# Expert rows summed by group in PSUM with one-hot products instead of through memory

## The chip, the cores and the metric

One Trainium2 chip, one of its cores. The time is the device time of one execution in microseconds (us). The trace is of one profiled execution; PE is the matrix engine, DVE, ACT and POOL are the vector, scalar and GpSimd engines, SP issues most DMAs.

## The reference, cut to what matters

One encoder layer (Hyena and HGRN2 mixers, an output projection, a mixture of experts, a final norm) on 1024 tokens and 16 meta tokens, width 1024, all float32. The change lies in the experts and in what follows them. 64 experts stand in 8 groups of 8; a token goes to the two best experts of its best group, so both its experts are in one group.

```python
# h: tokens after the mixers; hf = rms_norm(h) * gain
g_sel = argmax(hf @ w_rg);  top 2 of the 8 experts of that group, gates p_group * p_top / sum(p_top)
y_e   = (silu(xe @ w_gate[e]) * (xe @ w_up[e])) @ w_down[e]        # 1024 -> 512 -> 1024
out   = rms_norm(h + sum over the token's two experts of gate * y_e) * norm_final
```

Each expert has three matrices of 2 MB, 403 MB in all. They are read once.

## The kernel before, in words

The mixers take the first 780 us and are not touched. Then come three stages.

Routing (`choose`, `route`, `rows_out`, `gates`). The last output projection is woven with the choice of experts. Each of the eight 128-token tiles of h goes to memory (`rdr`, L1180) with its rsqrt factor in an extra column. `route` makes, with one-hot bf16 products on PE, a table of 64 slots for each expert: which row to fetch (`tab.src`) and where to put the result (`tab.dst`).

Experts (the loop at L1735). For expert x, POOL fetches its rows by an indirect DMA (`xg`, L1345, five buffers): partitions 0 to 63 hold the first halves of 64 rows, 64 to 127 the second halves. PE transposes them (`xt`), multiplies gate and up side by side in the two column halves (`gu`, L1367: 16 float32 matmuls, which the trace records as two passes each), ACT scales, PE transposes (`ht`, L1372), ACT and DVE make silu times up (L1374, L1375), PE multiplies with w_down (`y`, L1385: 8 matmuls, two passes each), DVE copies, and POOL writes the rows by an indirect DMA to `yd` in memory (L1388). PE works in order: gu(x), ht(x), with xt(x+1) between, y(x), gu(x+1).

The matrices come in 2 MB transfers on SP's queue (L1320, L1328) into nine buffers, in the order gate, up, down. A transfer is issued when the second before it has landed (`AHEAD` = 2) and its buffer is free. The first seven are issued while the routing still runs; the eighth waits for the second row fetch to land ("rows first").

End (`overflow`, `final`). All engines read `over` and skip the branch for experts with more than 64 rows, which is not taken here. Then the 8 MB of `yd` are read back in eight tiles, each tile is summed with h by the gates (on PE for four tiles, on DVE for four), ACT sums the squares, POOL makes the rsqrt in six small operations, DVE scales, and SP writes the result.

## Time and profile before

| | us |
|---|---|
| median of 3 runs | 1871.41 (1870.23 to 1877.0) |
| the profiled execution, its own time | 1871.61 |
| its span | 1869.9 |
| routing ends, the eighth matrix is issued | 849.93 |
| the last matrix has landed, about | 1815.7 |
| end of the span | 1869.9 |

| in the span | PE | DVE | ACT | POOL |
|---|---|---|---|---|
| busy | 86% | 43% | 24% | 11% |

A row of a timeline has start, duration, engine, line, operation and tiles, and how many such instructions are merged in it; in square brackets stands the idle time before and what ended it. SPq and POOLq are the queues of those engines. A row of windows has the busy time of each engine in that stretch with its instructions, then PE's granted clock (1 is 2.4 GHz), the busy share of the 16 DMA engines and GB/s. A row of groups has total busy time and mean ns of one instruction.

### The profile page before, as it was taken

The numbers are of one execution on the slowest core, as the hardware profiler recorded it, in microseconds if no ns is written. First come the engines' busy times: TensorE is split into PE (matmuls) and PEld (weight loads), VectorE is DVE, ScalarE is ACT, GpSimd is POOL, SyncE is SP. The second block draws the span as 40 slices with busy tenths as digits, with TensorE's granted clock in tenths as the row PEclk, the third lists the DMA queues.
The fourth block names the chain that finished last, engine by engine and source line by source line (L and its number), as shares of the span: only waits on it lengthen the run. The fifth ranks groups of instructions, "written<-read, shape, count | busy, mean of one in ns | idle before, by whom it ended". The sixth has DMA issues, their size and how long they took to land. (4 is left out here: it accounts for less than half of the span.)

```text
span 1869.9 us, 23041 instructions
## 1 busy us (share of the span) xinstructions
PE 1615.8 (86%) x8931; PEld 988.5 (53%) x8931; DVE 812.5 (43%) x1633; ACT 455.6 (24%) x871; POOL 203.5 (11%) x271
## 2 busy tenths in 40 slices
PE   5999999989998898998988888888888888888885
PEld 3998988878886676873332222222222232223232
DVE  6688879869889785671111111111111111111114
ACT  5443346353454552231000000000000000000001
POOL 0011000000100001002111111111111111111004
PEclk9999999999998898998999999999999999999997
DMA  5376766676745526468999999999999999999987
GB/s 168 94 225 196 233 194 201 206 223 195 212 161 179 181 72 151 160 271 355 424 420 419 420 418 420 421 421 421 422 420 420 417 420 419 421 422 416 412 357 283
DMA packets 150057, 574.55 MB, mean 307 GB/s; under 512 B 20468, under 2 KB 85072, under 8 KB 124153
## 3 DMA queue, kind: packets, MB, share of 16 engines
q1 hardware_dynamic: 122840, 511.30, 69.3%
q0 software_dynamic: 25808, 57.00, 10.4%
q10 hardware_dynamic: 1296, 4.75, 0.6%
q8 instruction: 71, 1.16, 0.2%
q14 instruction: 42, 0.34, 0.1%
HBM read 532.79 MB, written 57.02 MB: 315 GB/s over the span
## 5 line engine op out<-in xcount | busy, mean ns | idle before, releaser
L1367 PE MATMUL gu<-w,xt 128*64 128x512 f32 x2048 | 516.0, 604 | 76.3 <-DMA w<-in_w_up 75.5
L1367 PEld LDWEIGHTS gu<-w,xt 128*64 128x64 f32 x2048 | 167.6, 139 | 407.9 <-issue 278.9
L1362 DVE TENSOR_TENSOR xt<-xt,gain 128x512 f32<-128x512 f32 x64 | 44.2, 691 | 526.6 <-PE gu L1367 489.1
L1385 PE MATMUL y<-w,ht 128*64 128x512 f32 x1024 | 236.4, 602 | 25.8 <-DVE ht L1375 25.4
L1369 ACT ACTIVATE gu<-gu,xg 128x512 f32<-128x512 f32 x64 | 44.0, 687 | 849.3 <-PE gu L1367 849.3
L496 PE MATMUL w<-ah,wh 128*128 128x346 f32 (+2 forms) x672 | 233.4, 348 | 0.7 <-ACT ah L248 0.7
L496 PE MATMUL w<-al,wh 128*128 128x346 f32 (+2 forms) x672 | 234.0, 348 | 0.0
L496 PE MATMUL w<-ah,wl 128*128 128x346 f32 (+2 forms) x672 | 232.9, 348 | 0.0
L1385 PEld LDWEIGHTS y<-w,ht 128*64 128x64 f32 x1024 | 69.4, 137 | 151.0 <-issue 112.1
L1387 DVE COPY y<-y 128x512 f32<-128x512 f32 x64 | 44.2, 691 | 241.5 <-PE y L1385 241.5
L496 PEld LDWEIGHTS w<-ah,wh 128*128 128x128 f32 x672 | 128.3, 191 | 11.0 <-issue 1.6
L496 PEld LDWEIGHTS w<-ah,wl 128*128 128x128 f32 x672 | 128.5, 192 | 9.9 <-issue 1.6
L496 PEld LDWEIGHTS w<-al,wh 128*128 128x128 f32 x672 | 128.4, 191 | 9.0 <-issue 1.2
L1345 POOL DMA_INDIRECT xg<-rdr,src x64 | 65.6, 1024 | 485.0 <-ACT gu L1369 474.7
L1388 POOL DMA_INDIRECT yd<-y,dst x64 | 65.1, 1017 | 371.1 <-DVE y L1387 368.2
L1372 PE MATMUL ht<-ident,gu 128*128 128x128 f32 x256 | 47.7, 309 | 50.2 <-ACT gu L1369 50.1
L1372 PEld LDWEIGHTS ht<-ident,gu 128*128 128x128 f32 x256 | 35.6, 208 | 103.1 <-ACT gu L1369 103.1
L1375 DVE TENSOR_TENSOR ht<-ht 128x256 f32<-128x256 f32 x64 | 27.0, 421 | 94.8 <-ACT ht L1374 86.4
L498 ACT ACTIVATE pc<-w 128x346 f32<-128x346 f32 (+2 forms) x84 | 41.9, 499 | 72.2 <-PE w L496 67.1
L462 PE MATMUL h<-fh,ftab 128*128 128x256 f32 x256 | 53.0, 288 | 4.7 <-ACT fh L449 3.6
L486 ACT CAST wh<-w 128x512 fp32r<-128x512 f32 x64 | 39.5, 620 | 63.0 <-PE w L496 56.4
L1360 PE MATMUL xt<-ident,xg 128*128 128x128 f32 x256 | 42.9, 290 | 11.5 <-DMA xg<-rdr,src 10.5
(427 smaller groups left out, 2269.0 us busy)
## 6 DMA issues: line engine op xcount, KB each, us to landing
w<-in_w_gate SPq DMA_DIRECT2D x64, 2048.0 KB
w<-in_w_down SPq DMA_DIRECT2D x63, 2048.0 KB
w<-in_w_up SPq DMA_DIRECT2D x62, 2048.0 KB
w<-in_w_in SPq DMA_DIRECT2D x64, 256.0 KB
ftab<-in_tab POOLq DMA_DIRECT2D x32, 384.0 KB, 4.3
tab<-in_tabf POOLq DMA_DIRECT2D x16, 768.0 KB, 5.8
tab<-in_tabi POOLq DMA_DIRECT2D x16, 640.0 KB
kdr<-V SPq DMA_DIRECT2D x16, 512.0 KB
```

Source lines behind the costliest of these rows:

```text
L462: nc.tensor.matmul(A[-1][:, z * HC:z * HC + HC], lhs, rhs, start=i == 0, stop=i == len(prods) - 1)
L496: nc.tensor.matmul(pt[:, :n], lhs[k // 4][:, k % 4, :], rhs[:, k, c0:c0 + n], start=i == 0, stop=i == 3 * KT - 1)
L498: nc.scalar.activation(dst[:, c0:c0 + n], pt[:, :n], func)
L1345: d = nc.gpsimd.indirect_dma_start(out=xg, out_offset=None, in_=rows, in_offset=bass.IndirectOffsetOnAxis(ap=src, axis=0), bounds_check=2 ...
L1360: nc.tensor.transpose(pt[:, j].rearrange("p h s -> p (h s)"), xg[:, j:512:4], e.ident)
L1362: nc.vector.tensor_mul(xt, pt, gain[:, :, :, None].to_broadcast([P, 4, 2, SLOTS]))
L1367: nc.tensor.matmul(pg[64 * z:64 * z + 64], xt[:, j, h], w[:, h, j], start=i == 0, stop=i == 7)
L1369: nc.scalar.activation(gu, pg, AF.Copy, scale=xg[:, 512:513])
L1372: nc.tensor.transpose(pu[:, j].rearrange("p h s -> p (h s)"), gu[:, j::4], e.ident)
L1385: nc.tensor.matmul(py[64 * z:64 * z + 64], ht[:, j], wdv[:, j, z], start=j == 0, stop=j == 3)
L1387: nc.vector.tensor_copy(y, py)
L1388: nc.gpsimd.indirect_dma_start(out=ydv, out_offset=bass.IndirectOffsetOnAxis(ap=dst, axis=0), in_=y, in_offset=None, bounds_check=4 * SEQ ...
```

## The change

Weights: gate and up of an expert lie side by side in memory, one run of 32 KB for each partition, and come as one 4 MB transfer into one of three buffers; w_down has three buffers of 2 MB. The order is gate+up, down, expert by expert; the last four are gate+up 62 and 63, down 62 and 63. Four transfers (14 MB, as before) are issued ahead of "rows first".

Results: `expert_add` multiplies an expert's result by its gates and adds h itself for a token's first expert (`res`), splits it in two float32r parts (`yh`, `yl`), and 8 one-hot float32r products of 64 rows each (`hot`) add it to the group's sums in PSUM (two tiles of 128 tokens, four banks). Four of the eight stand after gu of the next expert, four after its `ht`; xt(x+1) and then y(x) follow. After the eighth expert of a group `group_out` normalises the sums (rsqrt by 13 small DVE operations) and POOL writes them to the result by token. `yd`, its reading back and `final` remain only in the branch for overflow, which now stands at the very end.

Tables: `group_tables`, after `gates`, makes the place of each slot in its group, its gate, whether it is the token's first expert, and the token of each place. The PSUM tiles gu, ht and y have one buffer each (two before).

```diff
     oh, m = first_max(e, rp, gl, c.rev, "g")
+    nc.vector.tensor_copy(c.G[:, ts], oh)
     t4 = rp.tile([P, n, 8, 8], F32, name="t4", bufs=1)
...
+GROUP = 256
+
+
+def group_tables(e, ps, rp, kp, c, tab):
+
...
+    Gf = c.G.rearrange("p t g -> p (t g)")
+    pg = ps.tile([P, 512], F32, name="t")
+    nc.tensor.matmul(pg[:, :64], c.tri, Gf, start=True, stop=False)
+    for i in range(1, 8):
+        nc.tensor.matmul(pg[:, i * 8:64], c.ones, Gf[:, :(8 - i) * 8], start=False, stop=i == 7)
...
+    def by_slot(values, out, first, last):
+
+        r = rp.tile([P, 2, 8, NE], BF16, name="rg", bufs=2)
+        for k in range(2):
+            nc.vector.tensor_mul(r[:, k], c.E[:, k], values[k][:, :, None].to_broadcast([P, 8, NE]))
+        for k in range(2):
+            for t in range(8):
+                nc.tensor.matmul(out, c.hot[:, k, t], r[:, k, t], start=first and k + t == 0, stop=last and k + t == 8)
+
+    pq = ps.tile([P, 512], F32, name="f")
+    by_slot((q[:, 1], q[:, 1]), pq[:, :NE], True, True)
+    tab.q = e.room[0][:, :NE]
+    nc.vector.tensor_scalar(tab.q, pq[:, :NE], -1.0, None, op0=ALU.add)
...
+    for i in range(3):
+        part = rp.tile([P, 2, 8], BF16, name="gp", bufs=2)
+        nc.vector.tensor_copy(part, rem if i else c.w)
+        if i < 2:
+            nc.vector.tensor_sub(rem, rem if i else c.w, part)
+        by_slot((part[:, 0], part[:, 1]), pw[:, :NE], i == 0, i == 2)
+    tab.ws = e.room[0][:, NE:]
+    nc.vector.tensor_copy(tab.ws, pw[:, :NE])
...
+    pt = ps.tile([P, 512], F32, name="f")
+    for h in range(GROUP // P):
...
+        hq = rp.tile([P, 2, 8, NE], BF16, name="rg", bufs=2).rearrange("p k t x -> p (k t x)").rearrange("p (t c) -> p t c", c=P)
+        nc.vector.tensor_tensor(hq, places[:, None, :].to_broadcast([P, 8, P]), qh[:, :, None].to_broadcast([P, 8, P]),
+                                op=ALU.is_equal)
+        for t in range(8):
+            nc.tensor.matmul(pt[:, 16 * h:16 * h + 16], hq[:, t], rt[:, t].rearrange("p j g -> p (j g)"),
+                             start=t == 0, stop=t == 7)
...
 AHEAD = 2
 XB = 5
-RD = 7
-ORDER = (2, 3, 0, 5, 1, 7, 8, 4, 6)
...
+RD = 4
+GU = [("gu", x) for x in range(NE)]
+DN = [("d", x) for x in range(NE)]
+LOADS = GU[:2] + DN[:1] + GU[2:3] + DN[1:3] + [l for x in range(3, NE - 2) for l in (GU[x], DN[x])] + GU[NE - 2:] + DN[NE - 2:]
...
+    kind, x = LOADS[i]
+    if kind == "gu":
+        w = pools["gu"][x % 3].tile([P, 2, 2, 4, 512], F32, name="wgu")
+        src = I["w_gu"][x]
+        if x == NE - 1:
+            for h in range(2):
+                d = nc.sync.dma_start(w[:, h], src[:, h])
         else:
-            d = nc.sync.dma_start(w, src)
+            d = nc.sync.dma_start(w.rearrange("p h z j f -> p (h z j f)"), src.rearrange("p h z j f -> p (h z j f)"))
...
+        w = pools["d"][x % 3].tile([P, 2, 4, 512], F32, name="w")
         if x == NE - 1:
-            nc.sync.dma_start(dst[:, 0], src[:, 0])
-            d = nc.sync.dma_start(dst[:, 1], src[:, 1])
+            src = I["w_down"][0, x].rearrange("(p h j) c -> p h (j c)", h=2, j=2)
+            for h in range(2):
+                d = nc.sync.dma_start(w[:, h].rearrange("p j f -> p (j f)"), src[:, h])
...
     nc = e.nc
     pt = ps.tile([P, 4, 2, SLOTS], F32, name="xt")
     for j in range(4):
-        nc.tensor.transpose(pt[:, j].rearrange("p h s -> p (h s)"), xg[:, j:512:4], e.ident)
+        last = nc.tensor.transpose(pt[:, j].rearrange("p h s -> p (h s)"), xg[:, j:512:4], e.ident)
     xt = xp.tile([P, 4, 2, SLOTS], F32, name="xt")
     nc.vector.tensor_mul(xt, pt, gain[:, :, :, None].to_broadcast([P, 4, 2, SLOTS]))
+    return xt, last
+
+
+def expert_hidden(e, ps, xp, wgu, xg, xt, between=None):
+
+    nc = e.nc
     pg = ps.tile([P, 512], F32, name="gu")
     for i in range(8):
         h, j = divmod(i, 4)
-        for z, w in enumerate((wg, wu)):
-            nc.tensor.matmul(pg[64 * z:64 * z + 64], xt[:, j, h], w[:, h, j], start=i == 0, stop=i == 7)
+        for z in range(2):
+            last = nc.tensor.matmul(pg[64 * z:64 * z + 64], xt[:, j, h], wgu[:, h, z, j], start=i == 0, stop=i == 7)
     gu = xp.tile([P, 512], F32, name="gu")
     nc.scalar.activation(gu, pg, AF.Copy, scale=xg[:, 512:513])
     pu = ps.tile([P, 4, 2, SLOTS], F32, name="ht")
-    for j in range(4):
-        nc.tensor.transpose(pu[:, j].rearrange("p h s -> p (h s)"), gu[:, j::4], e.ident)
+    with ExitStack() as order:
+        if between:
+            with e.tc.issue_after(last.ins):
+                last = between(0)
+            order.enter_context(e.tc.issue_after(last.ins))
+        for j in range(4):
+            last = nc.tensor.transpose(pu[:, j].rearrange("p h s -> p (h s)"), gu[:, j::4], e.ident)
+    if between:
+        with e.tc.issue_after(last.ins):
+            between(1)
     ht = xp.tile([P, 4, SLOTS], F32, name="ht")
     nc.scalar.activation(ht, pu[:, :, 0], AF.Silu)
     nc.vector.tensor_mul(ht, ht, pu[:, :, 1])
...
+def expert_add(e, ps, xo, wd, ht, xg, x, tab, acc):
+
+
+    nc = e.nc
+    wdv = wd.rearrange("p h j f -> p (h j f)").rearrange("p (j z c) -> p j z c", j=4, z=2)
+    one = slice(x, x + 1)
+    res = xo.tile([P, 512], F32, name="res", bufs=2)
+    nc.vector.tensor_scalar(res, xg[:, :512], tab.first[:, one], None, op0=ALU.mult)
+    hot = xo.tile([P, GROUP], F32R, name="hot", bufs=2)
+    nc.vector.tensor_scalar(hot, e.places, tab.q[:, one], None, op0=ALU.is_equal)
+    py = ps.tile([P, 512], F32, name="y")
+    for j in range(4):
+        for z in range(2):
+            nc.tensor.matmul(py[64 * z:64 * z + 64], ht[:, j], wdv[:, j, z], start=j == 0, stop=j == 3)
+    nc.vector.scalar_tensor_tensor(res, py, tab.ws[:, one], res, op0=ALU.mult, op1=ALU.add)
+    yh = xo.tile([P, 512], F32R, name="yh", bufs=2)
+    nc.scalar.copy(yh, res)
+    yl = xo.tile([P, 512], F32R, name="yl", bufs=2)
+    nc.vector.tensor_sub(yl, res, yh.bitcast(F32))
+
+    def products(c):
+        for z in range(2):
+            r = slice(64 * z, 64 * z + 64)
+            for i, y in enumerate((yh, yl)):
+                last = nc.tensor.matmul(acc[c][:, z], hot[r, c * P:c * P + P], y[r], start=x % 8 + i == 0, stop=x % 8 == 7 and i == 1)
+        return last
+    return products
+
+
+def group_out(e, xo, acc, gain, tok, out):
+
+    nc = e.nc
+    n = GROUP // P
+    ss = xo.tile([P, n], F32, name="fs")
+    for c in range(n):
+        junk = xo.tile([P, 2, 512], BF16, name="fj")
+        nc.scalar.activation(junk, acc[c], AF.Square, accum_out=ss[:, c:c + 1])
+    r = rsqrt(e, xo, ss, D)
+    for c in range(n):
+        y = xo.tile([P, 2, 512], F32, name="fo", bufs=2)
+        nc.vector.scalar_tensor_tensor(y, acc[c], r[:, c:c + 1], gain, op0=ALU.mult, op1=ALU.mult)
+        nc.gpsimd.indirect_dma_start(out=out, out_offset=bass.IndirectOffsetOnAxis(ap=tok[c], axis=0),
+                                     in_=y.rearrange("p h c -> p (h c)"), in_offset=None, bounds_check=SEQ - 1, oob_is_err=False)
+
...
+        ch.close()
+        xh = pool(c6, "xh", 2)
         xp = pool(c6, "xp", 2)
...
+        xo.tile([P, 3360], mybir.dt.uint8, name="pad")
+        gu = [pool(c6, "gu1"), pool(c6, "gu0")]
+        dn = [pool(c6, "d1")] + [pool(c6, f"d{i}", side="right") for i in (0, 2)]
+        gu.append(pool(c6, "gu2", side="right"))
+        we = {"gu": [gu[1], gu[0], gu[2]], "d": [dn[1], dn[0], dn[2]]}
+        e.wdma, e.W = [], {}
+        at = 0
+        for at in range(RD):
+            expert_weights(e, we, at)
...
             rdv = rdr.rearrange("t h c -> (t h) c")
-            ydv = yd.rearrange("t k (h c) -> (t k h) c", h=2)
...
+            e.places = xo.tile([P, GROUP], F32, name="places")
+            nc.gpsimd.iota(e.places, pattern=[[1, GROUP]], base=0, channel_multiplier=0, allow_small_or_imprecise_dtypes=True)
+            fgain = xo.tile([P, 2, 512], F32, name="fg")
+            nc.scalar.dma_start(fgain.rearrange("p h c -> p (h c)"), I["norm_final"].rearrange("(o d) -> o d", o=1).to_broadcast([P, D]))
+            accs, due = {}, {}
+
+            def close(x, c):
+
+                last = due[x](c)
...
+            def down(x, ht):
+                g = x // 8
+                if g not in accs:
+                    accs[g] = [ps.tile([P, 2, 512], F32, name="acc") for _ in range(GROUP // P)]
+                due[x] = expert_add(e, ps, xo, e.W["d", x], ht, rows[x][0], x, tab, accs[g])
+
+            hts = {}
+            xt, _ = expert_rows(e, ps, xh, rows[0][0], gain)
             for x in range(NE):
-                while len(W) < min(3 * x + 9, 3 * NE):
-                    W.append(expert_weights(e, we, len(W)))
+                while at < min(2 * x + 6, 2 * NE) or x >= NE - 2 and at < 2 * NE:
+                    expert_weights(e, we, at)
+                    at += 1
+                hts[x] = expert_hidden(e, ps, xh, e.W["gu", x], rows[x][0], xt, (lambda c: close(x - 1, c)) if x - 1 in due else None)
+                if x < NE - 1:
+                    xt, last = expert_rows(e, ps, xh, rows[x + 1][0], gain)
...
-                    late.append(expert_hidden(e, ps, xp, W[g], W[g + 1], rows[x][0], gain))
+                    with tc.issue_after(last.ins):
+                        down(x, hts.pop(x))
                 if x + XB < NE:
                     rows.append(fetch(e, xp, tab.src[:, x + XB:x + XB + 1], rdv, False))
-            for x, ht in zip((NE - 2, NE - 1), late):
-                expert_out(e, ps, xp, W[2 * NE + x], ht, tab.dst[:, x:x + 1], ydv)
-        c6.close()
+                if x == 4:
+                    over = nc.values_load(tab.over[0:1, 0:1], min_val=0, max_val=8 * SEQ)
+            for x in (NE - 2, NE - 1):
+                down(x, hts.pop(x))
+            for x in (NE - 2, NE - 1):
+                for c in range(2):
+                    close(x, c)
+        op = Room([we["gu"][i].tile([P, 2, 2, 4, 512], F32, name="wgu").rearrange("p h z j f -> p (h z j f)") for i in range(3)]
+                  + [we["d"][i].tile([P, 2, 4, 512], F32, name="w").rearrange("p h j f -> p (h j f)") for i in range(3)])
+        ydv = yd.rearrange("t k (h c) -> (t k h) c", h=2)
         with ExitStack() as c2:
-            overflow(e, psum(c2, xt=1, gu=1, ht=1, y=1), pool(c2, "op"), tab, gain, rdv, ydv)
-        fps = ctx.enter_context(tc.tile_pool(name="fps", bufs=1, space=PSUM, reuse_waits="tile"))
-        final(e, pool(ctx, "fp", 2), fps, hres, yd, tab.w, out)
+            ps = psum(c2, xt=1, gu=1, ht=1, y=1)
+            with tc.If(over > 2 * GROUP):
+                overflow(e, ps, op, tab, gain, rdv, ydv)
+                final(e, op, rdr, yd, tab.w, out)
 
 
```

## Rows read from the trace of the kernel before

**Rows 1.** Windows: the stretch in which experts are loaded, and the end behind it.
```profile
849.93:1815.70 965.77, 812.67 (x3554) 301.66 (x3556) 113.76 (x190) 69.85 (x129) 126.07 (x124) 0.99 1.01 419
1815.70:1869.90 54.20, 29.68 (x78) 11.65 (x74) 23.48 (x27) 8.83 (x16) 19.79 (x50) 0.79 0.64 250
```
**Rows 2.** Waits of SP's queue, 900 to 1800 us: total us, times, longest.
```profile
SPq L1320 <- DMA w<-in_w_up: 286.0, 57, 6.2
SPq L1328 <- DMA w<-in_w_gate: 262.4, 57, 5.4
```
**Rows 3.** Timeline of SP's queue: two issues of matrices, one after the other.
```profile
1302.48 0.33 SPq L1320 DMA_DIRECT2D w<-in_w_up  x1
1307.34 0.33 SPq L1328 DMA_DIRECT2D w<-in_w_down  x1
```
**Rows 4.** Timeline of PE: one round of the expert loop while weights are ahead.
```profile
877.49 6.18 PE L1367 MATMUL gu<-w,xt 128*64 128x512 f32 x28
883.59 0.75 PE L1360 MATMUL xt<-ident,xg 128*128 128x128 f32 x4
884.53 0.74 PE L1372 MATMUL ht<-ident,gu 128*128 128x128 f32 x4 [0.18 <-ACT gu L1369]
885.20 1.08 PE L1367 MATMUL gu<-w,xt 128*64 128x512 f32 x4
886.20 3.65 PE L1385 MATMUL y<-w,ht 128*64 128x512 f32 x16
889.68 1.89 PE L1367 MATMUL gu<-w,xt 128*64 128x512 f32 x8
```
**Rows 5.** Timeline, first and last of 32 float32r products; group of their weight loads.
```profile
812.86 0.48 PE L1058 MATMUL f<-woll,ygh 128*128 128x512 f32 x1
820.05 0.39 PE L1058 MATMUL f<-wohl,ygl 128*128 128x512 f32 x1
...
L1058 PEld LDWEIGHTS f<-wohl,ygl 128*128 128x128 f32 x32 | 6.0, 188 | 1.2
```
**Rows 6.** Timeline: from gu to y within one expert.
```profile
1305.36 0.74 PE L1372 MATMUL ht<-ident,gu 128*128 128x128 f32 x4 [0.83 <-ACT gu L1369]
...
1307.04 3.65 PE L1385 MATMUL y<-w,ht 128*64 128x512 f32 x16 [0.45 <-DVE ht L1375]
```
**Rows 7.** Groups by line: total busy us, mean ns, idle before and its releasers.
```profile
L1045 DVE TENSOR_TENSOR wol<-hres,woh 128x512 fp32r<-128x512 f32 x8 | 5.1, 677 | 0.0
...
L1044 ACT CAST woh<-hres 128x512 fp32r<-128x512 f32 x8 | 4.6, 619 | 5.9 <-DMA hres<-in_w_out 5.9
...
L1518 ACT ACTIVATE fj<-f 128x1024 bf16<-128x1024 f32 x4 | 4.1, 1019 | 9.9 <-PE f L1512 8.6 <-POOL rqx L152 1.3
...
L1521 DVE SCALAR_TENSOR_TENSOR fo<-f,rqy,fg 128x1024 f32<-128x1024 f32 x4 | 5.1, 1284 | 6.4 <-POOL rqy L157 6.3
...
L123 DVE TENSOR_TENSOR rqt<-rqy 128x4 f32<-128x4 f32 x12 | 1.9, 159 | 0.2
```
**Rows 8.** Timeline: from the routing into the experts.
```profile
844.04 0.17 DVE L1237 TENSOR_TENSOR wts<-wts,low 128x8 f32<-128x8 f32 x1
...
846.53 1.02 POOL L1345 DMA_INDIRECT xg<-rdr,src  x1 [0.30 <-issue]
...
849.93 0.34 SPq L1320 DMA_DIRECT2D w<-in_w_up  x1
...
850.46 8.89 PE L1367 MATMUL gu<-w,xt 128*64 128x512 f32 x32 [0.78 <-DVE xt L1362]
...
863.26 0.33 SPq L1320 DMA_DIRECT2D w<-in_w_up  x1
```
**Rows 9.** Timeline: the last two y, the last store of POOL, the last scaling.
```profile
1814.68 7.09 PE L1385 MATMUL y<-w,ht 128*64 128x512 f32 x32
...
1823.18 0.99 POOL L1388 DMA_INDIRECT yd<-y,dst  x1 [2.85 <-DVEq L1399]
...
1864.17 1.28 DVE L1521 SCALAR_TENSOR_TENSOR fo<-hres,rqy,fg 128x1024 f32<-128x1024 f32 x1 [1.09 <-POOL rqy L157]
```

## What the change will do to the time, predicted blind

> **What bounds the kernel now.** I read four views in this order. The windows by stage come first: from 849.93 us to about 1815.7 us the 16 DMA engines are busy throughout at 419 GB/s, while PE is busy 813 of 966 us, and the last 54.2 us run at 250 GB/s with little of anything [rows 1]. The waits of SP's queue say that this middle stretch is bound by the transfers: nearly every issue waits for an earlier matrix to land, not for a buffer [rows 2]. The timeline of that queue gives the pace of a matrix alone: 4.86 us for 2.097 MB, 431 GB/s [rows 3]. The timeline of PE where weights are ahead gives its own pace: 889.68 - 877.49 = 12.2 us for an expert [rows 4]. The three matrices of an expert take 14.6 us alone, and 965.8 us / 185 matrices x 3 = 15.66 us as measured [rows 1]. So DMA sets the stretch, and PE has some 3 us to spare for each expert. Behind the stretch nothing overlaps: finish y, write `yd`, read it back, sum, normalise, store.
>
> **The change part by part.** The sum is made on the profiled execution: span 1869.9 us, its own time 1871.61, so 1.7 us lie around the span; the median of the runs is 0.2 us lower.
>
> *The stretch of the weights.* 185 matrices at 4.86 us are 899 us of the 965.8; the other 67 us go to the indirect rows. By the code these are 1024 tokens x 2 experts x 4 KB = 8.4 MB of fetches and as much of `yd`, some 16.1 MB within the stretch: 241 GB/s, dearer than a matrix [rows 1, 3]. The change takes `yd` away and adds 4.2 MB of result rows, of which seven groups, 3.7 MB, fall into the stretch. Priced by its bytes at 431 GB/s `yd` is 19 us; if all the dearness is its own, 67 - 18 = 49 less what fetches cannot avoid, so I take half of 67, 34 us, as the upper end, and 25 as the value. The new stores cost 9 to 15 us, I take 11: their rows are 4 KB where those of `yd` were 2 KB. Net -14 us, bounds -25 and -4.
> One 4 MB transfer for two of 2 MB: a matrix alone already runs at 431 GB/s with the next one queued behind it, and DMA shows no idle time, so I cost it at nothing; what covers its start is the transfer before it, at least 4.86 us [rows 1, 3]. The Trainium skill, "DMA: Bandwidth & Descriptors", section "Anatomy of one DMA", gives each DMA a fixed 2 us, which would promise 128 us for 64 DMAs fewer; the rows show no such gap between two matrices, so the sum has none of it; by the page it would be 1703 us, to which the trace leaves no chance worth a number.
>
> *PE in the stretch.* An expert gains 8 products of 64 rows x 512 columns, float32r, and no other PE work. Such a shape is not in the trace; the nearest is the float32r product with 128 rows, (820.05 - 812.86) / 31 = 0.232 us each, its weight load of 0.188 us hidden [rows 5]. That makes 1.86 us; if the two row halves ran side by side, 0.93; if weight loads were not hidden, 8 x 0.42 = 3.4. I take 1.86. A change of operand shape also costs: a pair of gu passes over 512 columns takes 6.10 / 14 = 0.436 us, so four transposes of 128 columns about as much, an estimate; from 884.53 to the next gu at 885.20 it is 0.67, so 0.24 us [rows 4]. There are two such changes per expert now and five after: +0.7 us. From the 12.2 us goes the wait of 0.5 us of `ht` for ACT, which the first four products now fill (0.83 us between the end of gu and `ht`), and from `ht` to y there are 1.7 us, filled by four products and xt(x+1) [rows 4, 6]. So 12.2 - 0.5 + 1.9 + 0.7 = 14.3 us per expert, bounds 13.2 and 16. The DMA gives 64 experts about 959 us from the first gu to the last y (sum below), 15.0 each. PE stays just under; that margin, 0.7 us of 15, is the tightest point of this forecast. On DVE an expert gains four passes over 128 x 256 to 512 at up to 0.7 us and on ACT one of 0.62 [rows 7]: 3 us and 1.7 us of 15, off the path. `group_out` puts some 8 us on ACT and DVE once in eight experts; its sums must be free when the next group's first products come, a round later: it just fits, and a slip costs a few us per group on PE only. On POOL two stores per group stand ahead of later fetches, which have five buffers, so four rounds, of lead.
>
> *The start.* `choose` and `route` gain five small DVE operations (0.2 us) where DVE is full: +1 us on the way to "rows first". `group_tables` is twelve times a 128 x 512 pass of 0.68 us and some 15 small ones of 0.16 to 0.2: 11 us of DVE [rows 7]. Some runs in gaps; I put 9 us behind the gates, ready at 844.04. Before, gu(0) starts at 850.46 [rows 8]; after, it waits for DVE until about 853.5, bounds 850 and 859. It takes 8.9 us, to 862.4. The third gate+up buffer is full by then, so the next transfer waits for gu(0) to end, and the queue runs dry at 863.26, when before the second of the two matrices issued at 850 lands [rows 8]. So up to 4 us of delay are covered by those two matrices; I take +4 us in all for a cover that frays, bounds 0 and +10.
>
> *The end.* With T the landing of the last matrix, about 1815.7 before, the last y ends at T + 6.1 [rows 9]. After, y of expert 63 waits for the sum of 62 to be read (one PSUM buffer): T + 7. Then one by one: scale and add 0.7, cast 0.62, difference 0.68 and hand-offs (T + 9.3), four products 0.9 (T + 10.2), two sums of squares at 1.02 + 0.2 (T + 12.7), 13 small operations at about 0.2 (T + 15.3), two scalings of 1.28 (T + 17.9) [rows 5, 7]. The store is indirect, on POOL; the last one before goes from 1865.45 to 1869.9, 4.4 us, by SP [rows 9]. I take 5 us and 0.6 for the branch: T + 23.5, bounds 20 and 28, in place of 54.2 [rows 1]. Net -30.7, bounds -34 and -26.
>
> **Sum.** 1869.9 + 4 - 14 - 30.7 = 1829.2 us of span, and 1.7 around it: **1831 us**. The bounds added up give 1813 and 1851.
>
> **The rivals.**
> *PE becomes the bound, slower than before.* The products do not hide their weight loads, because each half of the rows is used twice running: 8 x 0.188 = 1.5 us more per expert, a cycle of 15.8. The end is then 853.5 + 64 x cycle + 16.5 (from the last y) + 1.7. At 15.8 it is 1883; with 0.2 us more for the five changes of shape, 1896. It decides from a cycle of 15.0, and the kernel is slower than before from 15.62. For it: no 64-row product of this width is in the trace, and the margin is thin. Against: 31 products in a row hid loads of the same size [rows 5], and the rounds have two places in which PE waits today. Two pages stand for it. The Trainium skill, "TensorE: Matmul & The Clock Gate", section "Part 3: Packing small matmuls", lets a weight load overlap a running matmul only in another row group; the rows differ, since full-height loads are hidden at 0.232 us. "TensorEngine Tiling (Array Packing)" of the skill, section "Key Properties", says that a change of tiling mode drains the engine; the 0.24 us agrees in kind.
> *PE slightly over.* Cycle 15.0 to 15.5: 1832 to 1864, say 1850.
> *The start starves.* The tables hold gu(0) until 859 and the fetches slip by 3 us: +10 in place of +4 and no more, since afterwards the transfers run on: 1837; with half the gain of `yd`, 1845.
> *The large transfers help.* If matrices ran at 4.86 us less what the fetches disturb, and stores cost nothing, another 15 us go: about 1815.
>
> **How the numbers follow.** Forecast (DMA stays the bound) 0.74, within 1815 to 1846; start and rows dearer, 1845 to 1855, 0.06; PE slightly over 0.09; PE the bound and slower 0.07; below 1815 0.04. The range 1814 to 1857 leaves out the slow case and the edges. A difference under 0.5% (9 us, 1862 to 1881) cannot be told from no change here. Faster 0.89: the forecast, the start, the large transfers and half of PE slightly over; same 0.04; slower 0.07.
>
> **What would show it.** Right: DMA share still 1.0 from 850 us to about 1806, SP's queue waiting for matrices, PE waiting for gate+up once per expert, products at 0.23 us or less, 22 to 25 us from the last landing to the end. Wrong: PE without idle time in the stretch and SP's queue waiting for gu or y (a cycle over 15.0); DMA idle between 860 and 870 us by more than 4 us (the start); GB/s in the stretch not above 419 for matrices and fetches alone (then `yd` was cheaper than 25 us); a store at the end that takes 8 us, not 5.

## The result and the profile after

The changed kernel takes 1840.82 us (median of 4 runs, 1840.11 to 1841.27) where the kernel before took 1872.24 in the same session: a ratio of 0.983 (95% interval 0.981 to 0.985), 31 us or 1.7% faster. The profiled execution has a span of 1838.9 us and a time of its own of 1840.71, so 1.8 us lie around the span. The forecast was 1831 (1814 to 1857): right in sign and in what sets the bound, 10 us too fast, and these 10 us are what is left of three misses of 8 to 9 us each.

The windows of the kernel after, from the start of the weights to the end (columns as in [rows 1]; the last three are granted clock, DMA share, GB/s):

```profile
850.00:855.00 5.00, 2.29 (x32) 1.93 (x33) 4.48 (x14) 0.00 (x0) 0.75 (x2) 0.50 0.27 105
855.00:860.00 5.00, 2.00 (x34) 1.48 (x31) 4.03 (x9) 0.00 (x0) 2.28 (x3) 0.50 0.00 1
860.00:865.00 5.00, 2.02 (x6) 1.03 (x8) 1.57 (x3) 0.00 (x0) 4.40 (x6) 0.50 0.54 133
863.01:1807.00 943.99, 866.60 (x4042) 341.58 (x4042) 237.78 (x481) 122.13 (x218) 75.97 (x77) 0.99 1.00 424
1807.00:1838.90 31.90, 11.11 (x51) 4.30 (x50) 7.78 (x20) 3.87 (x8) 2.01 (x2) 0.73 0.06 24
```

The fourth row is the stretch: the DMA engines are full for 944 us at 424 GB/s, PE is busy 867 of them (813 of 966 before, [rows 1]). The last row is the end, 31.9 us with the DMA engines nearly idle (share 0.06). The first three rows are the start, and here is what the forecast did not have: little is transferred from 850 us on and nothing between 855 and 860. SP's queue waits, as before, for matrices to land and not for buffers (waits of SP's queue, 860 to 1830 us):

```profile
SPq L1395 <- DMA wgu<-in_w_gu: 569.6, 59, 10.6
SPq L1403 <- DMA w<-in_w_down: 281.4, 59, 6.0
```

So the transfers are still the bound [rows 2]. One round of PE where the weights are ahead (timeline of PE):

```profile
892.14 7.04 PE L1450 MATMUL gu<-wgu,xt 128*64 128x512 f32 x32
899.10 0.50 PE L1507 MATMUL acc<-yh,hot 64*128 64x512 f32 x2
899.44 0.40 PE L1507 MATMUL acc<-yl,hot 64*128 64x512 f32 x2
900.01 0.75 PE L1460 MATMUL ht<-ident,gu 128*128 128x128 f32 x4 [0.17 <-ACT gu L1452]
900.69 0.51 PE L1507 MATMUL acc<-yh,hot 64*128 64x512 f32 x2
901.03 0.40 PE L1507 MATMUL acc<-yl,hot 64*128 64x512 f32 x2
901.36 0.75 PE L1437 MATMUL xt<-ident,xg 128*128 128x128 f32 x4
902.04 3.65 PE L1496 MATMUL y<-w,ht 128*64 128x512 f32 x16
905.53 1.46 PE L1450 MATMUL gu<-wgu,xt 128*64 128x512 f32 x6
```

From gu to gu 905.53 - 892.14 = 13.39 us (12.2 before, [rows 4]); the stretch gives 944 / 64 = 14.75 for each expert. The eight products stand in two gaps, 899.10 to 900.01 (0.17 of it a wait) and 900.69 to 901.36: 1.41 us in all. In the code (`products`) `yh` and `yl` on rows 0 to 63 come first, then `yh` and `yl` on rows 64 to 127. The trace starts both `yh` first (899.104 and 899.111) and then both `yl` (899.441 and 899.445): the two halves of the rows run side by side, and a row of two products lasts 0.50 us where one product on all rows lasted 0.48 [rows 5].

The start on POOL (timeline; in brackets the idle time before and what ended it):

```profile
823.14 0.60 POOL L1297 DMA_DIRECT2D edr<-E  x1 [30.16 <-DVE rqt L139]
849.94 0.34 POOL L1874 IOTA places<- 128x256 f32 x1 [26.19 <-DMA rdr<-hres]
850.22 0.53 POOL L1419 MEMSET xg<- 128x516 f32 x1
857.10 0.53 POOL L1419 MEMSET xg<- 128x516 f32 x1 [6.35 <-DVE rg L1363]
857.94 1.36 POOL L1420 DMA_INDIRECT xg<-rdr,src  x1 [0.31 <-POOL xg L1419]
859.61 1.02 POOL L1420 DMA_INDIRECT xg<-rdr,src  x1 [0.30 <-issue]
```

The operation of DVE that the second memset waits for (timeline of DVE):

```profile
855.83 1.22 DVE L1363 TENSOR_TENSOR rg<-gs,gq 128x1024 bf16<-128x1024 bf16 x1
```

The transfers behind the fetches (timeline of SP's queue):

```profile
863.01 0.81 SPq L1403 DMA_DIRECT2D w<-in_w_down  x2
873.80 0.33 SPq L1395 DMA_DIRECT2D wgu<-in_w_gu  x1
```

The last rows of h land at 849.94. The second memset of a row buffer `xg` waits 6.35 us until L1363 has read `gq`, a small tile of `group_tables`; by the addresses of the program `gq1` (bytes 40096 to 40160 of a partition) lies inside that buffer (38400 to 40464). Both first fetches stand behind this memset in POOL's order, and the two gated weight transfers behind the fetches: 863.01 us, where the eighth matrix before went at 849.93 [rows 8].

The end, first the y of the last expert (timeline of PE):

```profile
1812.24 3.65 PE L1496 MATMUL y<-w,ht 128*64 128x512 f32 x16 [0.84 <-DVE res L1497]
```

Its scaling, and the scaling of the group's two sums (timeline of DVE):

```profile
1815.95 0.75 DVE L1497 SCALAR_TENSOR_TENSOR res<-y,cvrows,res 128x512 f32<-128x512 f32 x1 [2.38 <-PE y L1496]
1823.69 2.48 DVE L1523 SCALAR_TENSOR_TENSOR fo<-acc,rqy,fg 128x1024 f32<-128x1024 f32 x2
```

The first sum of squares (timeline of ACT):

```profile
1818.95 1.02 ACT L1519 ACTIVATE fj<-acc 128x1024 bf16<-128x1024 f32 x1 [1.55 <-PE acc L1507]
```

The two stores (timeline of POOL):

```profile
1825.25 1.02 POOL L1524 DMA_INDIRECT out<-fo,cvrows  x1 [86.08 <-DVE fo L1523]
1830.42 0.99 POOL L1524 DMA_INDIRECT out<-fo,cvrows  x1 [4.16 <-issue]
```

The chain to the scaling `fo` goes as forecast. Then the second store of the group, whose input is ready at 1826.2, is issued only at 1830.42, 4.16 us after POOL was done with the first, and the span ends 8.5 us later. In the chain that ended last, the first store's landing lies between the two (to 1828.57):

```profile
1825.25 3.32 DMA out<-fo,cvrows
```

The trace also holds POOL's closing instructions, which the views leave out, and they split the 8.5 us: the second store has landed by 1833.20, 2.8 us after its issue; then POOL takes 1.10 us to post the landing on a semaphore and 3.74 us for a closing DRAIN instruction, to 1838.07; 0.8 us of closing waits follow. In the kernel before, SP issues the last store, and the same DRAIN of POOL (3.64 us, 1863.90 to 1867.54) runs beside that store. The second store here moves nothing: the trace has 125 packets of 4 KB behind the first and none behind the second, because the rows of the last group fit into one tile.

### The profile page after: what moved, and what is told of

Its sections match the earlier page's. It is cut to its first block, busy times and chain, and to the rows that moved or that the text cites. A ratio compares the mean times of both kernels' runs of the same rounds, so it can differ in the third digit from the quotient of the medians.

```text
span 1838.9 us, 24153 instructions
## 1 busy us (share of the span) xinstructions
PE 1657.8 (90%) x9483; PEld 1026.7 (56%) x9483; DVE 932.9 (51%) x1955; ACT 502.8 (27%) x951; POOL 136.3 (7%) x177
## 4 chain that ended last, share of the span: by engine, by line
issue 44%; PE 25%; DMA 11%; DVE 6%; POOL 4%; ACT 1%; POOLq 0%; SPq 0%; DVEq 0%; ACTq 0%
PE w L498 12%; DMA out<-fo,cvrows 7%; POOL xg L1420 3%; PE wo L1060 2%; DMA g<-udr 2%; PE h L656 1%; PE f L983 1%; PE h L609 1%; PE wo L1140 1%; PE f L953 1%; PE h L464 1%; PE f L1060 1%; PE u L920 1%; DMA wr<-in_w_router_expert 1%; DMA wn<-in_win 1%
## 5 line engine op out<-in xcount | busy, mean ns | idle before, releaser
L1450 PE MATMUL gu<-wgu,xt 128*64 128x512 f32 x2048 | 463.7, 605 | 66.9 <-DMA wgu<-in_w_gu 65.6
L1450 PEld LDWEIGHTS gu<-wgu,xt 128*64 128x64 f32 x2048 | 164.0, 139 | 328.6 <-issue 325.2
L1497 DVE SCALAR_TENSOR_TENSOR res<-y,cvrows,res 128x512 f32<-128x512 f32 x64 | 48.0, 750 | 195.7 <-PE y L1496 195.7
L1499 ACT CAST yh<-res 128x512 fp32r<-128x512 f32 x64 | 39.5, 617 | 327.1 <-DVE res L1497 327.1
L1437 PEld LDWEIGHTS xt<-ident,xg 128*128 128x128 f32 x256 | 39.5, 207 | 66.4 <-issue 62.4
L1501 DVE TENSOR_TENSOR yl<-res,yh 128x512 fp32r<-128x512 f32 x64 | 44.3, 692 | 45.7 <-ACT yh L1499 45.6
L1507 PE MATMUL acc<-yh,hot 64*128 64x512 f32 x256 | 65.0, 495 | 0.4 <-ACT yh L1499 0.4
L1437 PE MATMUL xt<-ident,xg 128*128 128x128 f32 x256 | 61.1, 331 | 3.7 <-DMA xg<-rdr,src 2.9
L1507 PEld LDWEIGHTS acc<-yh,hot 64*128 64x128 f32 x256 | 24.6, 183 | 59.5 <-issue 51.1
```

Of the source, the lines that this page charges most:

```text
L1437: last = nc.tensor.transpose(pt[:, j].rearrange("p h s -> p (h s)"), xg[:, j:512:4], e.ident)
L1450: last = nc.tensor.matmul(pg[64 * z:64 * z + 64], xt[:, j, h], wgu[:, h, z, j], start=i == 0, stop=i == 7)
L1497: nc.vector.scalar_tensor_tensor(res, py, tab.ws[:, one], res, op0=ALU.mult, op1=ALU.add)
L1501: nc.vector.tensor_sub(yl, res, yh.bitcast(F32))
L1507: last = nc.tensor.matmul(acc[c][:, z], hot[r, c * P:c * P + P], y[r], start=x % 8 + i == 0, stop=x % 8 == 7 and i == 1)
```

## The experiments

All runs are variants of the changed kernel unless said. A variant's time stands beside the kernel before of its own session (1869.7 to 1872.1 in all of them). Because what lies ahead of the routing varies from run to run by several us, the stages are also read from each profile between fixed events: "rows" is from POOL's store of the router's table (`edr`, 823.14 above) to the landing of the last rows (849.94; for the kernel before, to the first fetch), "gate" from there to the first gated transfer (863.01), "stretch" from there to the first slice of 1 us in which the DMA share is under 0.5 (1807), "end" from there to the end of the span.

| run | rows | gate | stretch | end | sum | median us |
|---|---|---|---|---|---|---|
| before | 23.5 | 4.9 | 966.1 | 53.9 | 1048.3 | 1872.24 |
| b_again (before) | 23.5 | 4.9 | 964.5 | 51.2 | 1044.0 | 1870.64 |
| after | 26.8 | 13.1 | 944.0 | 31.9 | 1015.8 | 1840.82 |
| a_again (after) | 26.8 | 13.2 | 944.0 | 31.1 | 1015.2 | 1841.82 |
| a_start | 26.8 | 6.5 | 945.6 | 31.7 | 1010.6 | 1836.08 |
| a_views | 26.8 | 12.9 | 945.1 | 26.7 | 1011.5 | 1832.44 |
| a_both | 26.8 | 6.3 | 947.3 | 27.2 | 1007.6 | 1835.03 |
| a_two_2mb | 27.1 | 13.1 | 949.2 | 30.1 | 1019.5 | 1843.94 |
| a_halves | 27.1 | 13.2 | 945.7 | 32.5 | 1018.5 | 1840.28 |
| a_yd2 | 26.8 | 13.0 | 970.8 | 32.0 | 1042.5 | 1865.62 |
| a_no_out | 26.8 | 13.2 | 935.0 | 33.7 | 1008.7 | 1833.90 |
| a_prod2 | 26.8 | 13.0 | 945.1 | 31.4 | 1016.3 | 1841.24 |

"Rows" ends at another event in the kernel before, so between the two kernels only rows and gate together compare strictly: 28.3 us before, 39.9 after. The stretch ends on a whole us, so a difference under 1 us in it or in the end says nothing. The two traces of after and a_again agree within 1 us in each stage; the two of the kernel before differ by 1.6 us in the stretch and 2.7 in the end. Medians move more, since `edr` itself moves (823.14 in after, 818.23 in a_views, 813.62 in a_both): small differences are read from the stages.

**Base and noise: a_again, b_again.** No edit.

> The changed kernel itself, as the base of the other runs of this chip. Both theories: 1836 to 1842 us. From the landing of the last row store (the end of POOL's wait for it) to the issue of the first two gated weight transfers 13.1 us, as in the profile after.

> The kernel before itself, for a second trace of it. Theory: what lies ahead of the store of the router's table (821.59 us in its first trace, 813.6 to 823.1 in those of the changed kernel's variants) varies from run to run and is no part of the change; from there to the first fetch it takes 23.5 us again, and from the first fetch to the eighth matrix 4.9 us. Rival: it lies within 1 us of 821.6 again, and the later start of the changed kernel is the change's own.

a_again: 1841.82 us (1838.81 to 1845.05), gate 13.2: as expected. b_again: 1870.64, and its trace shows (timeline of POOL)

```profile
823.18 0.61 POOL L1290 DMA_DIRECT2D edr<-E  x1 [30.00 <-DVE rqt L139]
846.67 1.15 POOL L1345 DMA_INDIRECT xg<-rdr,src  x1 [9.20 <-DVE wts L1237]
```

`edr` at 823.18, not 821.59 as in its first trace, and in the variants of the changed kernel between 813.62 and 823.14: this point moves by itself, and 1.5 us of the changed kernel's later start are no part of the change. From `edr` to the first fetch it is 23.49 us in both traces of before; in those of the changed kernel `edr` to the landing is 26.8 (27.1 in two). These 3.3 us are the change's own (the ends are a fetch and a landing, see above).

**The start: a_start.**

```diff
-PAD = 66488
+PAD = 66232
...
+    rp.tile([P, 640], mybir.dt.uint8, name="pad", bufs=1)
     t = rp.tile([P, 8, 8], F32, name="gt", bufs=1)
...
-    rp.tile([P, 384], mybir.dt.uint8, name="pad", bufs=1)
```

> The changed kernel with the small tiles gt and gq1 of group_tables moved past the address range of the second row buffer xg (the pad stands ahead of them and is 640 bytes long). Theory: POOL's second memset of xg waits 6.35 us for the last reader of gq1, and both first fetches stand behind it in POOL's order; without that wait the fetches issue at about 851 and the first two weight transfers behind them at about 856 instead of 863.01; everything after is bound by the transfers, so the whole of it comes through: 1834 us (1833 to 1836). Rival: the fetches then wait for something as late (the table work on DVE that ends at 859.4 us, or the row store that lands at 849.9), and the time stays within 2 us of 1840.8.

Measured: 1836.08 us (1833.53 to 1842.01). The start on POOL (timeline of a_start):

```profile
849.22 1.14 POOL L1418 MEMSET xg<- 128x516 f32 x2
850.52 1.12 POOL L1419 DMA_INDIRECT xg<-rdr,src  x1 [0.17 <-POOL xg L1418]
851.95 1.14 POOL L1419 DMA_INDIRECT xg<-rdr,src  x1 [0.30 <-issue]
```

And on SP's queue:

```profile
855.42 0.81 SPq L1402 DMA_DIRECT2D w<-in_w_down  x2
869.89 0.33 SPq L1394 DMA_DIRECT2D wgu<-in_w_gu  x1
```

The wait is gone, the fetches and the gated transfers go some 6.5 us earlier after the landing (gate 6.5 for 13.1), so the cause of that part of the start is shown. But of these 6.6 the stretch gives back 1.6, so that the sum falls by 5 and the median ends just above the range that was expected: the third transfer now comes 14.5 us after the first two, which take 2 x 4.86 = 9.7 us [rows 3]. For 6.1 us of that SP's queue waits for gu(0) on PE. What is left of the gate beside the 4.9 us from the first fetch to the transfers, as in the kernel before, is 1.6 us: the iota (from 848.93) and the two memsets, which POOL now does between the landing and the first fetch.

**The end: a_views.**

```diff
+            outs = dram_disjoint_views(out[0], 2)
...
-        nc.gpsimd.indirect_dma_start(out=out, ...
+        nc.gpsimd.indirect_dma_start(out=outs[c], ...
```

> The changed kernel with the two stores of each group written through two views of the result that are taken as disjoint, so that the second does not wait for the landing of the first. Theory: in the last group the second store issues 4.2 us earlier (1830.42 becomes about 1826.3) and the end, 8.5 us after it, moves as much: 1836.5 us (1835.5 to 1838). In the stretch POOL's 46 us of waits go and change nothing, since POOL is off the path. Rival A: the landing of a store, not its issue, is what the end waits for, and two stores side by side land as late as one after the other: no change (1840 to 1841.5). Rival B: POOL's waits in the stretch did delay fetches of rows: 1830 or less.

Measured: 1832.44 us (1829.19 to 1833.7). The two last stores (timeline of POOL; the span ends at 1829.7):

```profile
1820.22 1.02 POOL L1525 DMA_INDIRECT out<-fo,cvrows  x1 [85.53 <-DVE fo L1524]
1821.89 0.99 POOL L1525 DMA_INDIRECT out<-fo,cvrows  x1 [0.65 <-DVEq L1921]
```

The second store is issued 1.67 us after the first (5.17 before) and the end is 4.4 to 5.2 us shorter; the stretch is as long as before. So the wait was the order that the program keeps between two stores to one tensor, and the waits of the same kind in the stretch cost nothing. The median fell by 8.4 us, outside every range that was expected; 4 to 5 us of it are the end, and most of the rest lies ahead of `edr` (818.23 us here, 823.14 in after), so rival B has nothing from it. The rows of the two stores never coincide here; how the branch that rewrites the result would be ordered behind them was not looked at.

**Both: a_both.** The two edits together.

```diff
...
+    rp.tile([P, 640], mybir.dt.uint8, name="pad", bufs=1)
     t = rp.tile([P, 8, 8], F32, name="gt", bufs=1)
...
+            outs = dram_disjoint_views(out[0], 2)
...
```

> The changed kernel with both mends: gt and gq1 out of the range of the second xg buffer, and the two stores of a group through disjoint views. Theory: the two waits lie one behind the other on the path (6.5 us ahead of the stretch and 4.2 us behind it), so that they add: 10 to 11 us less than the changed kernel on this chip. Rival: what the earlier start gives is lost in the stretch again (it began with fewer transfers done ahead and was 1.5 us longer in the first such run): 5 to 8 us less.

Measured: 1835.03 us (1823.01 to 1837.28), ratio 0.982 (0.979 to 0.985), a_again of the same session 0.986 (0.983 to 0.989). The median is 6.8 us under a_again, and by stages the sum is 7.6 to 8.2 us less than after: the rival, at its upper edge. The gate gives 6.9 and the end 4 to 5, and the stretch takes 3.3 back. Where, its windows show:

```profile
855.00:860.00 5.00, 5.00 (x20) 1.46 (x18) 0.00 (x0) 0.00 (x0) 0.00 (x0) 0.75 0.80 335
860.00:865.00 5.00, 4.88 (x26) 2.16 (x23) 1.11 (x2) 2.35 (x3) 1.01 (x1) 1.00 0.50 152
```

Between 855 and 865 us the DMA engines stand still for some 3.5 of 10 us (shares 0.80 and 0.50). The two gated matrices have landed, and the next gate+up needs the buffer of expert 0, whose gu runs from 852.22 to 861.9 because its input waits behind the tables on DVE (timeline of PE; wait of SP's queue, 840 to 890 us):

```profile
852.22 9.70 PE L1450 MATMUL gu<-wgu,xt 128*64 128x512 f32 x32 [1.34 <-DVE xt L1439]
SPq L1395 <- PE gu L1450: 6.5, 1, 6.5
```

It also lasts 9.70 us where a later one lasts 7.04: after a start in which PE was busy 1.54 and 2.82 of 5 us (840 to 850) the granted clock is 0.50 (1.2 GHz) up to 855 us, 0.75 in the mean of the first of the two windows and 1.00 in the second. In the kernel after, the late gate hid this.

**One large transfer or two: a_two_2mb and a_halves.** Both load gate and up by halves; in a_two_2mb each half waits for the transfer two before it, in a_halves the two go together and the waits are those of after.

```diff
...
-            d = nc.sync.dma_start(w.rearrange(...), src.rearrange(...))
+            for h in range(2):
+                d = nc.sync.dma_start(w[:, h], src[:, h])
...
```

> The changed kernel with gate and up of an expert loaded as two transfers of 2 MB (runs of 16 KB to a partition) in place of one of 4 MB, each waiting for the transfer two before it, as in the kernel before: two transfers of 2 MB under way. The prediction costed the 32 KB run at nothing: 1841 us (1839 to 1843). Rival: the larger transfers brought the 10 us that the stretch is shorter than forecast: 1851 us (1847 to 1856).

> The changed kernel with gate and up as two transfers of 2 MB issued together (runs of 16 KB), with the same waits as the single one: as many bytes under way as after, in smaller transfers. In the run with two transfers of 2 MB under way the stretch was 5 us longer. Theory A, bytes under way: as the changed kernel, 0 to 1.5 us more in the stretch. Theory B, the length of the runs or the count of transfers: 4 to 6 us more.

Measured: a_two_2mb 1843.94 us (1838.89 to 1847.83), a_halves 1840.28 (1836.49 to 1845.7). The stretch is 949.2 and 945.7 us for 944.0: 5.2 and 1.7 us more (one trace each; those of unchanged weights lie between 944.0 and 945.1). Windows of the stretch of a_two_2mb:

```profile
857.78:1807.00 949.22, 856.28 (x4052) 323.12 (x4054) 238.21 (x482) 122.59 (x219) 76.10 (x76) 1.00 1.01 422
```

So the single transfer is worth about 5 us, half of what the rival asked, and most of it comes with the bytes (or the transfers) under way and not with the length of a run, as far as one trace each can tell: the 1.7 us of a_halves are hardly outside the scatter. The Trainium skill, "DMA: Bandwidth & Descriptors", section "Anatomy of one DMA", gives a fixed 2 us for a DMA, there of those that GpSimd issues. These are SP's, with others under way: 63 transfers more cost 5.2 us in a_two_2mb, 0.08 us each, and 1.7 in a_halves.

**The stores of yd: a_yd and a_yd2.** a_yd stored `res` itself (three buffers); a_yd2 copies y as the kernel before did.

```diff
+    nc.gpsimd.indirect_dma_start(out=ydv, out_offset=... tab.dst[:, one] ..., in_=res, ...)    # a_yd
...
+    y = xp.tile([P, 512], F32, name="y", bufs=3)    # a_yd2
+    nc.vector.tensor_copy(y, py)
+    nc.gpsimd.indirect_dma_start(out=ydv, out_offset=... tab.dst[:, one] ..., in_=y, ...)
```

> The changed kernel with the kernel before's store of each expert's rows to yd put back (an indirect store of res by tab.dst for each of the 64 experts; nobody reads it). The prediction's term: 16.8 MB at the stretch's rate plus what the traces gave to such stores, 25 us (19 by bytes alone, up to 34): 1866 us. If the 10 us by which the stretch was shorter than forecast is the stores' own price, it comes out at 34 us or more: 1875 us. If it is something else (the 4 MB transfers), 19 to 25 us: 1860 to 1866 us.

> The changed kernel with the kernel before's copy of y and store to yd put back, from a tile of its own with three buffers as there (the first form stored res, whose next writer stands early in DVE's queue and waited for the landing). Theory of the prediction: 25 us more than the changed kernel (19 to 34), all of it in the stretch. Rival: the stores' requests delay the rows of later experts or the weight transfers more than their bytes say, which would account for the 7 us by which the stretch is shorter than forecast and that the larger transfers do not explain: 32 us or more.

a_yd: 1925.25 us, 84 us more than after. That is no price of the bytes. The waits of its stretch (863 to 1870 us):

```profile
DVE res L1490 <- DMA yd<-res,dst: 495.0, 60, 15.5
```

L1490, the first writer of the next `res`, stands early in DVE's order, and it now waited 8 us for each expert until a store had landed, with everything of DVE behind it. The run tells what a store costs when its buffer is on the path, and nothing of the stretch.

a_yd2: 1865.62 us (1859.93 to 1871.76), 24 us over a_again. Its stretch is 970.8 us, 26.8 more than after, and the gate and the end are as in after: the forecast of 25 held, and the rival (32 or more) fell.

**The stores of the result: a_no_out.** The stores of groups 0 to 6 are left out, so only the last group's rows are written.

```diff
-        nc.gpsimd.indirect_dma_start(out=out, ...
+        if store:
+            nc.gpsimd.indirect_dma_start(out=out, ...
```

> The changed kernel without the stores of the result in groups 0 to 6 (3.7 of 4.2 MB; the rows of the last group alone are written). Theory of the prediction: out stores cost 11 us in the stretch (9 to 15), 7/8 of it 9.6 us: 9 to 10 us less than the changed kernel. Rival: they ride in gaps of the weight transfers and cost 0 to 4 us, which would be a part of the stretch's unforecast gain.

Measured: 1833.90 us (1831.47 to 1836.11), stretch 935.0: 9.0 us less, as forecast for seven groups (9.6). Its end is 2 us longer: POOL's closing DRAIN takes 5.99 us there, for 3.74 in after; what it waits for is not shown.

**PE's margin: a_prod2 and a_prod3.** Every product is done twice or three times.

```diff
-            for i, y in enumerate((yh, yl)):
+            for i, y in enumerate((yh, yh, yl, yl)):        # a_prod2
+            for i, y in enumerate((yh, yh, yh, yl, yl, yl)):  # a_prod3
```

> The changed kernel with every product done twice (yh, yh, yl, yl in place of yh, yl: eight more per expert). Theory: an expert takes PE 13.4 us where weights are ahead and the transfers 944 / 64 = 14.75 us, so the margin is 1.35 us; eight products more at 0.232 us each are 1.86 us, the cycle is 15.25 us, PE becomes the bound and the time grows by up to 64 x 0.5 = 32 us: 20 to 32 us more than the changed kernel. Rival: the products lie in PE's waits for the weights and for ACT anyway, and up to 16 per expert cost nothing: 0 to 5 us.

> The changed kernel with every product done three times (24 per expert). With 16 the cycle of PE where weights are ahead was 14.07 us, still under the 14.75 of the transfers, and eight products took 1.14 us, not 1.86. Theory: eight more make it 15.2 us, over the transfers' pace, so that PE becomes the bound: about 64 x 0.46 = 29 us more than the changed kernel (20 to 35), with PE without waits for wgu and SP's queue waiting for PE. Rival: the transfers' pace is not the bound that the margin is taken against, and a third helping is as free as the second: 0 to 5 us.

a_prod2: 1841.24 us (1837.22 to 1844.71), no change, against the theory. Its round (timeline of PE):

```profile
891.71 7.04 PE L1450 MATMUL gu<-wgu,xt 128*64 128x512 f32 x32
898.67 0.74 PE L1507 MATMUL acc<-yh,hot 64*128 64x512 f32 x4
899.24 0.63 PE L1507 MATMUL acc<-yl,hot 64*128 64x512 f32 x4
899.80 0.75 PE L1460 MATMUL ht<-ident,gu 128*128 128x128 f32 x4
905.78 1.03 PE L1450 MATMUL gu<-wgu,xt 128*64 128x512 f32 x4
```

Four products take 0.57 us, 0.14 each, not 0.232, and the round 14.07 us: still under 14.75. The expected sum was wrong in the price: on one half of the rows a product follows the one before it after 0.23 us, and the other half runs beside it. The eight more also fill the 0.17 us in which `ht` waited for ACT. a_prod3: 1924.76 us (1919.88 to 1926.67), 84 us more than after, where 29 were expected. Two starts of gu, one round apart (timeline of PE):

```profile
1311.24 7.09 PE L1450 MATMUL gu<-wgu,xt 128*64 128x512 f32 x32
1327.53 0.65 PE L1450 MATMUL gu<-wgu,xt 128*64 128x512 f32 x2
```

The waits of SP's queue in the same run (863 to 1880 us):

```profile
SPq L1395 <- DMA wgu<-in_w_gu: 337.5, 59, 9.3
SPq L1403 <- PE y L1496: 287.1, 58, 7.4
SPq L1395 <- PE gu L1450: 99.0, 47, 3.7
```

The round is 16.29 us, over 14.75, and now SP's queue also waits for PE's buffers, 386 us, while its waits for gate+up to land fall from 569.6 to 337.5. The formula of the rival fits: gu(0) starts at 857.7 in this trace, and 857.7 + 64 x 16.29 + 16.5 = 1916.8 for a span of 1918.1. So PE becomes the bound between rounds of 14.07 and 16.29 us; 14.75 lies between, and the changed kernel stands 1.36 us under it. Why the third helping costs 2.22 us and the second 0.68 can be read from the products of one gap (timeline of PE):

```profile
1318.26 1.07 PE L1507 MATMUL acc<-yh,hot 64*128 64x512 f32 x4
1319.52 0.96 PE L1507 MATMUL acc<-yl,hot 64*128 64x512 f32 x4
```

The code puts six products on one half of the rows ahead of six on the other. Of the first four `yh` the trace starts three alone (1318.260, 1318.595, 1318.826); the other half begins with the fourth, at 1318.833, 0.57 us late, and its last three `yl` run alone. In after and in a_prod2 the halves start within 0.02 us of each other. Two gaps of 0.57 us, and two products more on each half in each gap at 0.23, make 2.06 of the 2.22 us. What holds the second half back when six stand ahead of it, and not when four do, is not shown.

## Why the prediction was right, and where it was off

*The bound.* "DMA sets the stretch" held: full DMA engines to 1807, SP's queue waiting for landings, PE waiting for gate+up 43 times (65.6 us in all). a_prod3 shows the other side.

*The stretch, forecast -14, was -22* (966.1 to 944.0; -20.5 against b_again). By the experiments: `yd` -26.8 (forecast -25, between 19 by its bytes and 34, half of what the indirect rows cost), result rows +9.0 (+11), the large transfer -5.2 (0). The three sum up to -23.0. The step that failed is "I cost it at nothing": a matrix alone runs at 431 GB/s [rows 3], but that row is a quiet moment, and a_two_2mb with a_halves shows something to gain for more bytes under way; that it is gained beside the indirect rows is a guess. The rival "the large transfers help" had the transfers, but its 15 us, three times the size, also counted on stores that cost nothing, and those cost 9.0.

*The start, forecast +4, was +13.* 1.5 us are the run's own (b_again), 3.3 lie between `edr` and the last rows (forecast +1; DVE has ten operations of `group_tables` there, 2.9 us in all; no run takes them away), and 8.2 are the gate, 6.6 of which a_start takes away; the other 1.6 are the iota and the memsets on POOL. The step that failed is the list of who waits for the tables. It had DVE and gu(0); it left out POOL, whose memsets had been done at leisure before (and the first fetch issued at once, [rows 8]), and which now found its buffer at the address of a table. A trace of the kernel before cannot show that wait; the order on POOL with the addresses of new tiles beside old ones could have. The upper bound, +10, was too low for it. The other worry, gu(0) late behind DVE, was real but hidden behind this wait: it appears once the wait is gone, and takes back 1.6 us in a_start and 3.3 in a_both.

*The end, forecast T + 23.5, was T + 31.9.* The chain to the end of `fo` was forecast at T + 17.9 and came at T + 19.2 (1826.2). The step that failed is "I take 5 us and 0.6 for the branch", one store's worth: there are two, the second waits for the first to land (4.2 us, of which a_views takes 3.5 away), and from the last issue to the end it takes 8.5 us (7.8 with both under way), not 5.6. The row used was a direct store by SP [rows 9], and the forecast named an 8 us store as what would show it wrong. But the store itself lands in 2.8 us: what was left out is POOL's own closing, 1.10 and 3.74 us, which comes behind the landing when POOL issues the last store, and ran beside SP's store before.

*PE, forecast 14.3 us for an expert, was 13.39.* The gaps of the products take 1.41 us, where the forecast had 1.86 for the products and 0.7 for the changes of shape. The step that failed here is taking the products one after the other; the text had named the other case, "if the two row halves ran side by side, 0.93", and that is what the trace shows: 0.23 us on one half, as the row with all 128 rows gave [rows 5], and the halves start 0.01 us apart. "TensorEngine Tiling (Array Packing)" of the Trainium skill, section "Key Properties", says that different tiles can load weights and multiply in parallel, and the trace agrees. The other 0.48 us lie at the changes of shape, for which the same section names a drain: the first and the last product of a gap are followed after 0.33 us (899.10 to 899.44, 901.03 to 901.36), not 0.23, so some 0.1 us at each of the four changes where the forecast had 0.24; whether that is the drain is not shown. The wait for ACT is not filled, as the forecast had it with 0.5 us: 0.18 us before [rows 4], 0.17 after. The round closes as 12.19 + 0.91 + 0.67 (the two gaps) - 0.26 (xt, with the wait ahead of `ht` that stood there before) - 0.14 (gu, in one piece now) = 13.37 of 13.39. The margin that the text called its tightest point was 1.36 us, twice what it feared, so the two rivals of PE had less behind them than the 0.16 given.

*The sum.* The start is 9 over, the end 9 (54.2 became 32, not 23.5), the stretch 8 under: 10 us slower than 1831. Three misses of that size that half cancel are luck in the total; the bounds of the start and of the end were both overrun.

## What to carry to other kernels

When work is put ahead of an address range that another engine's prefetch will use, list every queue that writes there, not only the engine that computes: a 64-byte table under a buffer cost 6.6 us of start here, 5 of them in the total. This program orders a store by indices to one tensor behind the one before it even where the rows differ, which cost nothing under transfers and some 4 us at the tail. Ask also which engine issues the last store: POOL's closing came behind its landing here; a last store by SP was not tried in the changed kernel. Split the stretch, the start and the end at events that the change does not touch, and compare stages: here single runs of a_both spread over 14 us, while the stages of the changed kernel repeat within 1.

## What the runs showed of the hardware

Putting back 8.4 MB of stores by indices in 2 KB rows cost 26.8 us, 313 GB/s, while the result's rows of 4 KB, 3.7 MB, cost 9.0 us, 411 GB/s; the stretch as a whole moves 424. The length of a row alone was not tested, and the trace records both kinds in packets of 4 KB, those of `yd` with as many of 8 bytes beside them (2020 each). Float32r products on the two halves of the rows run side by side, each half at 0.23 us for a product, the price of one on all rows, with the weights loaded meanwhile; the first and the last of a run take 0.33. An indirect store issued last by POOL landed in 2.8 us, and the program ended 5.7 us behind the landing, 3.74 of them POOL's closing DRAIN; a direct store by SP took 4.4 us to the end [rows 9].
